# Right operands of a seven-product feed-forward made in four steps, memory's second product moved into the layer, down products over three banks

## The chip, the cores and the metric

The program runs on one core of one Trainium2 chip. The metric is the device time of one execution in microseconds (us); the figure for a kernel is the median of its runs. A core has five engines that work at the same time, each through its own list of instructions in the list's order: TensorE (PE in the profile; matrix products into PSUM banks), VectorE (DVE), ScalarE (ACT), GpSimd (POOL) and SyncE (SP, which issues DMA transfers here). An instruction starts when those before it on its engine have started and what it waits for is done, so one that waits holds up everything queued behind it.

## What is computed

A decoder of two layers over 512 tokens of width 1024, then a second block with sparse attention and retention, all in fp32. What the change touches is the feed-forward at the end of each of the two layers and the second of two small products on a "memory" of 256 rows:

```python
for i in range(DEPTH):                      # DEPTH = 2
    mem_kv = mem_n @ w_mem_kv[i]            # memory's product, 256 x 1024 by 1024 x 512
    ...                                     # layer 0: gated convolution, layer 1: banded attention
    x = x + jnp.concatenate([y_tok, y_mem], axis=-1) @ w_out
    h = rmsnorm(x, norm_ffn[i])
    x = x + (jax.nn.silu(h @ w_gate[i]) * (h @ w_up[i])) @ w_down[i]    # D_FF = 2816
return rmsnorm(x, final_norm)               # then second_block(...)
```

## The kernel before

**Precision.** Every fp32 operand is split in two: a rounded high part (`copy` on ACT, L70) and the difference (`lo_of` on DVE, L80). A product is three matmuls: high by high, low by high, high by low (`mm3`, L120 to L122). A weight tile arrives by DMA as raw fp32 (`wr`, 2 buffers), and becomes `wh` on ACT and `wl` on DVE (3 buffers each; `weights`, L103). A third matmul of a product waits for `wl`.

**Layout.** x stands as eight chunks of 128 features by 512 tokens. A block f of the feed-forward is 128 of the 2816 inner features: 22 blocks in groups of 4, 4, 4, 4, 3, 3 (`FFG`, L25).

**Plain blocks** (f = 0 to 4, `plain_gate_up`, L604): gate and up are two products of 24 matmuls by 512 columns each, into a `pp` and an `lg` bank. Behind them `z` (gate times the norm row R, DVE L73), silu on ACT, `u` (up times -R, DVE L76), `u*z` on POOL (L73), and the split into `acth`, `actl`. Block 0 also makes R from the sums of squares of x.

**Seven-product blocks** (f = 5 to 21, `gate_up`, L566): gate and up of a block and both halves of the tokens are taken as one 2 by 2 product, made with seven products of half the size (84 matmuls by 256 columns) instead of eight. It needs two sets of sums. The right operands, sums of the gained and normed x, are made once per layer (`halves`, L494): for each of four pairs of chunks two scaled chunks (`b`, DVE L76), four sums of 256 columns, one split of 256 and three of 512 columns (`B`, `Bh` on ACT; `Bl` and the like on DVE). The left operands are sums of the weights, made per block (`pair_weights`, L535: `a`, `s`). The seven products share three banks: U (`pp`, read in between by copies on ACT: `g`, `g`, `u`), Y and Z (`lg`).

**Down products.** The products with w_down of group g are spread over the blocks of group g+1, eight of them (four weight loads `i` by two output chunks `c`), called by `between` inside a block; those of the last group follow the loop. Each goes into a bank of the tag `tp` (2 banks) or `po` (1 bank) and is subtracted from x (DVE L638). Which block gets how many was `share` (L646): none before f = 4, then two each, and 3, 3, 2 in the groups of three blocks.

**Around it.** `run` (L1156) calls the feed-forward of layer 0, then the loads for a bias table, `mem_kv(1)` (memory's product for layer 1, L372) and the bias table, which ends in a broadcast of 2,304 KB through DRAM on POOL's queue (`band<-band`, L340). Then `layer_b` begins with two splits of each chunk of x (`gh`, `gl` and `g`), a sum of squares on POOL, and products with w_kv. After layer 1 `second` begins in a like way. The order of each engine's list is fixed at build time by a scheduler, which may put instructions of later code ahead.

Of the kernel before, what the change touches and what calls it, by code (L numbers as in the profile page):

```python
# [25 lines left out]
PLAIN = 5  # L26


class Build:
# [464 lines left out]
    def halves(self, x, R, gain):  # L494

        nc = self.nc
        tags = iter(["pa"] * 6 + ["pb"] * 10 + ["q"] * 4 + ["v"] * 8)
        spare = []  # L500

        def slot(name):
            tag = next(tags)
            if tag != "v":
                return self.slot(tag, F32R, name=name)
            if not spare:
                t = self.slot("v", F32R, (128, KWORDS), name)
                spare.extend([t[:, :512], t[:, 512:1024]])
            return spare.pop(0)

        sub = lambda out, a, b: nc.vector.tensor_tensor(out, a, b, op=ALU.subtract)
        sets = []
        for j in range(len(x) // 2):
            a, b, m, t = self.slot("t", name="b1"), self.slot("t", name="b2"), self.slot("s", name="m12"), self.slot("s", name="t34")
            for c, o in ((2 * j, a), (2 * j + 1, b)):
                self.stt(o, x[c], gain[:, c:c + 1], R, ALU.mult, ALU.mult)
            b11, b12, b21, b22, m1, m2, t3, m4 = (o[:, u:u + 256] for o in (a, b, m, t) for u in (0, 256))
            one = slot("B11")
            self.copy(one[:, :256], b11)
            self.lo_of(one[:, 256:], b11, one[:, :256])  # L520
            sub(m1, b11, b12)
            self.stt(m2, b22, -1.0, m1, ALU.mult, ALU.subtract)
            sub(t3, b22, b12)
            self.stt(m4, m2, -1.0, b21, ALU.mult, ALU.subtract)
            parts = []
            for o in (b, m, t):
                h, l = slot("Bh"), slot("Bl")
                self.copy(h, o)
                self.lo_of(l, o, h)
                parts.append(((h[:, :256], l[:, :256]), (h[:, 256:], l[:, 256:])))  # L530
            (p21, p22), (p1, p2), (p3, p4) = parts
            sets.append([(one[:, :256], one[:, 256:]), p21, p1, p2, p3, p22, p4])
        return [[s[i] for s in sets] for i in range(7)]

    def pair_weights(self, src):  # L535

# [28 lines left out]

    def gate_up(self, src, B, between):  # L566

        nc, w = self.nc, self.pair_weights(src)
        mm = nc.tensor.matmul
        b11, b21, m1, m2, t3, b22, m4 = B  # L570

        def product(ps, a, b, start):
            for j in range(4):
                (ah, al), (bh, bl) = (a[0][:, j], a[1][:, j]), b[j]
                mm(ps, ah, bh, start=start and j == 0, stop=False, skip_group_check=not start)  # L575
                mm(ps, ah, bl, start=False, stop=False, skip_group_check=not start)  # L576
                mm(ps, al, bh, start=False, stop=j == 3, skip_group_check=not start)  # L577

        U, Y, Z = (self.psum(t)[:, :256] for t in ("pp", "lg", "lg"))
        g, u = self.slot("t", name="g"), self.slot("t", name="u")[:, :256]  # L580
        g1, g2 = g[:, :256], g[:, 256:]
        add = lambda out, a, b: nc.vector.tensor_tensor(out, a, b, op=ALU.add)  # L582
        product(U, w["a11"], b11, True)
        self.copy(g1, U)
        product(Y, w["a12"], b21, True)
        add(g1, Y, g1)
        product(U, w["s2"], m2, False)
        self.copy(g2, U)
        product(Z, w["s1"], m1, True)
        product(U, w["s3"], t3, False)  # L590
        self.copy(u, U)
        add(u, Z, u)
        between(0)
        product(Z, w["s4"], b22, False)
        add(g2, Z, g2)
        nc.scalar.activation(g, g, AF.Silu)  # L596
        product(U, w["a22"], m4, False)
        between(1)
        act = self.slot("t", name="act")
        self.mul(act[:, :256], U, g1)  # L600
        self.mul(act[:, 256:], u, g2)
        return self.split(act, "b", name="act")
# [14 lines left out]
        self.mul(u, u, z, self.nc.gpsimd)  # L617
        return self.split(u, "b", name="act"), R

    def ffn(self, layer):  # L620
        nc, T = self.nc, self.T
        gain = self.gain(2 + layer)
        h = self.gained(self.x, gain)
        R = B = act = None

        def down(i, act, g):

            f0, f1 = FFG[g]
            n = f1 - f0
            w = []  # L630

            def one(c):
                if not w:
                    w.extend(self.weights(T["w_down"][layer, i][:, f0 * 256:f1 * 256], 2 * n, 128))
                ps = self.psum("po" if i % 2 else "tp")
                self.proj(ps, None, act, [t[:, c * n:c * n + n] for t in w])
                x = self.x[2 * i + c]
                nc.vector.tensor_tensor(x, x, ps, op=ALU.subtract)  # L638

            return [lambda: one(0), lambda: one(1)]  # L640

        for g, (f0, f1) in enumerate(FFG):
            last = act
            todo = [] if last is None else [p for i in range(4) for p in down(i, last, g - 1)]
            act = []
            share = -(-len(todo) // (f1 - max(f0, PLAIN - 1))) if todo else 0  # L646
            for f in range(f0, f1):
                mine = []
                if f >= PLAIN - 1:
                    mine, todo = todo[:share], todo[share:]  # L650

                def between(i):
                    for p in mine[i * (len(mine) // 2):] if i else mine[:len(mine) // 2]:
                        p()

                if f < PLAIN:
                    a, R = self.plain_gate_up(layer, f, h, R)
                    between(0)
                    between(1)
                    if f == 0:  # L660
                        B = self.halves(self.x, R, gain)
                else:
                    a = self.gate_up(T["w_gu"][layer, f - PLAIN], B, between)
                act.append(a)
        for i in range(4):
            for p in down(i, act, len(FFG) - 1):
                p()
# [488 lines left out]
    def run(self):  # L1156
        self.load_consts()
        self.mrs = None
        self.layer_a()
        self.ffn(0)  # L1160
        loaded = self.bias_loads()
        self.mem1 = self.mem_kv(1)
        self.bias_tables(loaded)
        self.layer_b()
        self.ffn(1)
        self.second()
# [123 lines left out]
```

## Time and profile before

| | |
|---|---|
| median of 3 runs | 1707.94 us (1705.91 to 1709.22) |
| the profiled execution, its own time | 1709.18 us |
| its span, first to last instruction | 1707.3 us |
| mean granted TensorE clock | 0.979 of full speed |
| PE busy | 1629.6 us, 95% of the span |
| DVE busy | 1253.8 us, 73% |
| ACT busy | 757.4 us, 44% |
| POOL busy | 193.7 us, 11% |

The profiled execution is one execution. Its own time is 1.9 us more than its span; the 1.9 us lie before the first and after the last instruction. A row of the timeline gives the start in us from the span's start, the duration, engine, line, operation and tiles, and in brackets how long the engine stood idle before it and what ended that. Matmuls overlap in the pipeline, so what one costs is the step from its start to the next start, not its duration; DVE's and ACT's overlap by some hundredths in the same way. Clock is the share of full speed that TensorE was granted.

### The profile page before, as it was taken

To read this page: it belongs to the slowest core of one execution; us is meant where nothing else is said; L and a number is where in the kernel's file an instruction comes from. 1 tells how busy PE (TensorE), PEld (TensorE's weight loads), DVE (VectorE), ACT (ScalarE), POOL (GpSimd) and SP (SyncE) were. 2 spreads that over 40 slices of the span, in tenths; PEclk is the share of its full clock that TensorE was granted. 3 is DMA by queue.
4 is the path that set the end of the run, shared out by engine and by line. 5 is a ranking of instruction groups with operands and counts; after the bars stand their busy time and mean duration, and the time that the engine had idled before them with its cause. 6 is when DMAs were issued, how large, how long until landed. Compare 5 with 4: busy or idle time off the path is not lost.

```text
span 1707.3 us, 24407 instructions
## 1 busy us (share of the span) xinstructions
PE 1629.6 (95%) x9408; PEld 1423.0 (83%) x9408; DVE 1253.8 (73%) x2330; ACT 757.4 (44%) x1404; POOL 193.7 (11%) x186
## 2 busy tenths in 40 slices
PE   8999979999999899997999999989899999999997
PEld 6888868999998678886899999967787888888887
DVE  7866776777777969977677777689878977764444
ACT  6532344444444557734344444434555633333333
POOL 1112310000000600050100000051001001010010
PEclk9999989999999899998999999999999999999999
DMA  5222222332324441221323322332512022243352
GB/s 196 87 86 96 90 69 92 104 107 92 114 85 120 131 164 64 81 86 61 105 95 101 110 99 93 97 122 87 162 56 67 17 91 82 84 138 123 113 165 87
DMA packets 51572, 171.60 MB, mean 101 GB/s; under 512 B 6680, under 2 KB 6880, under 8 KB 51328
## 3 DMA queue, kind: packets, MB, share of 16 engines
q1 hardware_dynamic: 45504, 151.11, 27.2%
q0 software_dynamic: 5376, 18.82, 3.2%
q8 instruction: 74, 1.21, 0.3%
q14 instruction: 42, 0.34, 0.1%
q10 hardware_dynamic: 576, 0.11, 0.0%
HBM read 160.56 MB, written 11.81 MB: 101 GB/s over the span
## 4 chain that ended last, share of the span: by engine, by line
PE 72%; DVE 15%; DMA 5%; issue 3%; ACT 3%; POOL 1%; DVEq 0%; SPq 0%; ACTq 0%; POOLq 0%
PE pp L122 7%; PE pp L121 7%; PE pp L120 6%; PE lg L120 4%; DVE wl L80 4%; PE lg L122 4%; PE lg L121 4%; PE po L120 3%; PE pp L575 3%; PE pp L577 3%; PE pp L576 3%; PE po L121 3%; PE po L122 3%; DMA wr<-in_w_gu_dram 3%; PE tp L262 2%
## 5 line engine op out<-in xcount | busy, mean ns | idle before, releaser
L70 ACT ACTIVATE wh<-wr 128x1024 fp32r<-128x1024 f32 (+3 forms) x246 | 251.9, 1024 | 376.6 <-PE pp L121 150.5
L80 DVE TENSOR_TENSOR wl<-wr,wh 128x1024 fp32r<-128x1024 f32 (+3 forms) x246 | 315.9, 1285 | 63.3 <-ACT wh L70 62.6
L120 PE MATMUL pp<-g,wh 128*128 128x512 f32 x592 | 235.8, 399 | 21.9 <-DVE z L73 14.0
L122 PE MATMUL pp<-g,wl 128*128 128x512 f32 x592 | 235.0, 397 | 7.9 <-DVE wl L80 7.8
L121 PE MATMUL pp<-g,wh 128*128 128x512 f32 x592 | 234.4, 396 | 0.3 <-DVE g L76 0.3
L120 PEld LDWEIGHTS pp<-g,wh 128*128 128x128 f32 x592 | 112.5, 190 | 44.4 <-ACT Bh L70 14.7
L122 PEld LDWEIGHTS pp<-g,wl 128*128 128x128 f32 x592 | 112.1, 189 | 31.0 <-DVE wl L80 10.3
L121 PEld LDWEIGHTS pp<-g,wh 128*128 128x128 f32 x592 | 112.5, 190 | 21.4 <-DVE g L76 1.0
L70 ACT ACTIVATE s<-s 128x512 fp32r<-128x512 f32 x136 | 85.0, 632 | 49.2 <-DVE s L555 46.4
L80 DVE TENSOR_TENSOR s<-s,s 128x512 fp32r<-128x512 f32 x136 | 90.1, 682 | 1.0 <-ACT s L70 0.8
L575 PE MATMUL pp<-Bh,s 128*128 128x256 f32 x272 | 78.8, 290 | 7.3 <-ACT g L70 7.0
L555 DVE TENSOR_TENSOR s<-wr,wr 128x512 f32<-128x512 f32 x68 | 46.8, 688 | 51.9 <-DMA wr<-in_w_gu_dram 51.9
L577 PE MATMUL pp<-Bh,s 128*128 128x256 f32 x272 | 78.0, 287 | 0.0
L577 PE MATMUL lg<-Bh,s 128*128 128x256 f32 x272 | 77.0, 283 | 0.0
L575 PE MATMUL lg<-Bh,s 128*128 128x256 f32 x272 | 76.9, 283 | 0.0
L120 PE MATMUL po<-acth,wh 128*128 128x512 f32 x176 | 70.7, 401 | 5.8 <-DVE x L638 5.8
L121 PE MATMUL po<-actl,wh 128*128 128x512 f32 x176 | 70.1, 398 | 0.0
L122 PE MATMUL po<-acth,wl 128*128 128x512 f32 x176 | 69.3, 394 | 0.0
L120 PE MATMUL tp<-acth,wh 128*128 128x512 f32 x176 | 68.9, 391 | 0.0
L121 PE MATMUL tp<-actl,wh 128*128 128x512 f32 x176 | 68.9, 391 | 0.0
L122 PE MATMUL tp<-acth,wl 128*128 128x512 f32 x176 | 68.5, 389 | 0.0
L596 ACT ACTIVATE g<-g 128x512 f32<-128x512 f32 x34 | 21.4, 631 | 100.9 <-DVE g L582 100.9
(503 smaller groups left out, 4650.9 us busy)
## 6 DMA issues: line engine op xcount, KB each, us to landing
wr<-in_w_gu_dram SPq DMA_DIRECT2D x68, 512.0 KB, 3.8
wr<-in_w_in_dram SPq DMA_DIRECT2D x44, 512.0 KB, 3.5
wr<-in_w_down_dram SPq DMA_DIRECT2D x32, 512.0 KB, 3.7
wr<-in_a_w_in_dram SPq DMA_DIRECT2D x18, 512.0 KB, 3.6
wr<-in_w_down_dram SPq DMA_DIRECT2D x16, 384.0 KB, 3.2
wr<-in_w_gate_dram SPq DMA_DIRECT2D x10, 512.0 KB, 3.4
wr<-in_w_up_dram SPq DMA_DIRECT2D x10, 512.0 KB, 3.4
wr<-in_a_w_out_dram SPq DMA_DIRECT2D x8, 512.0 KB, 3.5
```

Source lines behind the costliest of these rows:

```text
L70: self.nc.scalar.activation(out, in_, AF.Copy, scale=scale)
L80: self.nc.vector.tensor_tensor(out, x, hi.bitcast(F32), op=ALU.subtract)
L120: mm(ps, ah, bh, start=start, stop=False)
L121: mm(ps, ah, bl, start=False, stop=False)
L122: mm(ps, al, bh, start=False, stop=stop)
L262: self.nc.tensor.transpose(ps[:, c:c + 128], src, self.ident)
L555: nc.vector.tensor_tensor(t, a, b, op=ALU.add)
L575: mm(ps, ah, bh, start=start and j == 0, stop=False, skip_group_check=not start)
L576: mm(ps, ah, bl, start=False, stop=False, skip_group_check=not start)
L577: mm(ps, al, bh, start=False, stop=j == 3, skip_group_check=not start)
L596: nc.scalar.activation(g, g, AF.Silu)
```

## The change

Four edits, all in the feed-forward and in `run`. (1) `halves` becomes a generator: one pair of chunks per step, one step behind each of the plain blocks 1 to 4, instead of all four behind block 0. (2) The down products of the first group are spread 4, 2, 1, 1 over blocks 4 to 7 instead of 2, 2, 2, 2; in the groups of three blocks 2, 3, 3 instead of 3, 3, 2. (3) Their banks go `tp`, `tp`, `po` in turn instead of `tp`, `tp`, `po`, `po`. (4) `mem_kv(1)` with the bias table moves from behind the feed-forward of layer 0 to a place ahead of its last eight down products.

```diff
@@ halves
             sets.append([(one[:, :256], one[:, 256:]), p21, p1, p2, p3, p22, p4])
-        return [[s[i] for s in sets] for i in range(7)]
+            yield sets
@@ ffn
-    def ffn(self, layer):
+    def ffn(self, layer, between_last=None):
...
-                ps = self.psum("po" if i % 2 else "tp")
+                ps = self.psum("po" if (2 * i + c) % 3 == 2 else "tp")
...
-            share = -(-len(todo) // (f1 - max(f0, PLAIN - 1))) if todo else 0
-            for f in range(f0, f1):
-                mine = []
-                if f >= PLAIN - 1:
-                    mine, todo = todo[:share], todo[share:]
+            n = f1 - f0
+            shares = [0] * n if last is None else [4, 2, 1, 1] if f0 < PLAIN else [8 * (i + 1) // n - 8 * i // n for i in range(n)]
+            for f, share in zip(range(f0, f1), shares):
+                mine, todo = todo[:share], todo[share:]
...
                 if f < PLAIN:
                     a, R = self.plain_gate_up(layer, f, h, R)
+                    if f == 0:
+                        steps = self.halves(self.x, R, gain)
+                    else:
+                        sets = next(steps)
                     between(0)
                     between(1)
-                    if f == 0:
-                        B = self.halves(self.x, R, gain)
                 else:
+                    if f == PLAIN:
+                        B = [[s[i] for s in sets] for i in range(7)]
                     a = self.gate_up(T["w_gu"][layer, f - PLAIN], B, between)
                 act.append(a)
+        if between_last:
+            between_last()
         for i in range(4):
@@ run
         self.layer_a()
-        self.ffn(0)
-        loaded = self.bias_loads()
-        self.mem1 = self.mem_kv(1)
-        self.bias_tables(loaded)
+        def between():
+            loaded = self.bias_loads()
+            self.mem1 = self.mem_kv(1)
+            self.bias_tables(loaded)
+
+        self.ffn(0, between)
```

What this does to the lists of the engines, at three places. First DVE's list in the plain blocks of layer 0, before: behind `u` of block 0 (here `u_1805`) all of `halves` follows, of which these are the first rows; `wl` is the difference of a weight tile, `actl` that of the block's result.

```order
L76 SCALAR_TENSOR_TENSOR u_1805<-lg_1774,Rf_345_1769 128x512
L76 SCALAR_TENSOR_TENSOR b_354_1812<-x_81,gains,Rf_345_1769 128x512
L76 SCALAR_TENSOR_TENSOR b_355_1813<-x_82,gains,Rf_345_1769 128x512
L511 TENSOR_TENSOR m_356_1814<-b_354_1812 128x256
L511 TENSOR_TENSOR t_357_1815<-b_355_1813,b_354_1812 128x256
L76 SCALAR_TENSOR_TENSOR m_356_1814<-b_355_1813,m_356_1814 128x256
L80 TENSOR_TENSOR wl_1983<-wr_1981,wh_1982 128x1024
L80 TENSOR_TENSOR actl_1809<-u_1805,acth_1808 128x512
```

Of the 41 rows between that `u` and `z` of block 1, 39 are of `halves`. The same list with the change, behind block 1's gate:

```order
L73 TENSOR_TENSOR z_1843<-pp_1812,Rf_345_1769 128x512
L80 TENSOR_TENSOR wl_1946<-wr_1944,wh_1945 128x1024
L76 SCALAR_TENSOR_TENSOR u_1877<-lg_1846,Rf_345_1769 128x512
L76 SCALAR_TENSOR_TENSOR b_366_1884<-x_81,gains,Rf_345_1769 128x512
L76 SCALAR_TENSOR_TENSOR b_367_1885<-x_82,gains,Rf_345_1769 128x512
L80 TENSOR_TENSOR actl_1881<-u_1877,acth_1880 128x512
L80 TENSOR_TENSOR B_370_1890<-b_366_1884,B_370_1890 128x256
```

Between `u` of a block and `z` of the next there stand now ten rows of one step, the block's `actl` and one `wl`, and a second `wl` behind that `z`. POOL's list has one instruction in each of these blocks, `u*z`.

Second, ACT's list around the first seven-product block of layer 0 (f = 5). Before, `g_2264` twice and `u_2265` are the copies out of bank U, and `wh_2402`, `a_477`, `s_479` and so on the left operands of block 6:

```order
L70 ACTIVATE wh_2332<-wr_2331 128x1024
L70 ACTIVATE wh_2402<-wr_2398 128x1024
L70 ACTIVATE g_2264<-pp_2261 128x256
L70 ACTIVATE a_477_2406<-wr_2399 128x512
L70 ACTIVATE s_479_2411<-s_478_2409 128x512
L70 ACTIVATE g_2264<-pp_2261 128x256
L70 ACTIVATE s_481_2416<-s_480_2414 128x512
```

With the change the left operands that stand around the copies are those of block 5 itself:

```order
L70 ACTIVATE s_458_2277<-s_457_2275 128x512
L70 ACTIVATE s_460_2282<-s_459_2280 128x512
L70 ACTIVATE g_2298<-pp_2295 128x256
L70 ACTIVATE s_462_2287<-s_461_2285 128x512
L70 ACTIVATE s_464_2292<-s_463_2290 128x512
L70 ACTIVATE g_2298<-pp_2295 128x256
L70 ACTIVATE wh_2366<-wr_2365 128x1024
L70 ACTIVATE u_2299<-pp_2295 128x256
L70 ACTIVATE wh_2436<-wr_2432 128x1024
L70 ACTIVATE a_482_2440<-wr_2433 128x512
```

`a_482`, the first that needs block 6's second raw tile, has moved behind all three copies.

Third, SP's list at the end of layer 0's feed-forward; before, the four loads of the last down products stand ahead of memory's weights (the last of the four is the second row):

```order
L355 DMA mem_5252<-in_mem_dram 128x512
L111 DMA wr_5214<-in_w_down_dram 128x768
L111 DMA wr_5275<-in_w_mem_k_dram 128x1024
L111 DMA wr_5318<-in_w_mem_k_dram 128x1024
L111 DMA wr_5360<-in_w_mem_v_dram 128x1024
L111 DMA wr_5366<-in_w_mem_v_dram 128x1024
```

With the change the four stand behind them, and the loads of w_kv still last:

```order
L111 DMA wr_5254<-in_w_mem_v_dram 128x1024
L111 DMA wr_5344<-in_w_down_dram 128x768
L111 DMA wr_5372<-in_w_down_dram 128x768
L111 DMA wr_5400<-in_w_down_dram 128x768
L111 DMA wr_5428<-in_w_down_dram 128x768
L111 DMA wr_5581<-in_w_kv_k_dram 128x1024
```

The last rows of memory's product on PE now stand ahead of the last eight down products, and the broadcast of the bias table ahead of the copies of x on POOL.

## Rows read from the trace of the kernel before

**Rows 1.** The page, part 1: busy us, share of the span, instructions of each engine.

```profile
PE 1629.6 (95%) x9408; PEld 1423.0 (83%) x9408; DVE 1253.8 (73%) x2330; ACT 757.4 (44%) x1404; POOL 193.7 (11%) x186
```

**Rows 2.** Timeline of PE, layer 0, plain blocks 1 to 4.

```profile
227.64 0.39 PE L121 MATMUL lg<-g,wh 128*128 128x512 f32 x1
235.00 0.77 PE L120 MATMUL pp<-g,wh 128*128 128x512 f32 x1 [6.97 <-DVE z L73]
...
238.59 0.79 PE L122 MATMUL lg<-g,wl 128*128 128x512 f32 x1 [2.40 <-DVE wl L80]
...
244.31 0.50 PE L120 MATMUL lg<-g,wh 128*128 128x512 f32 x1
...
251.49 0.39 PE L120 MATMUL lg<-g,wh 128*128 128x512 f32 x1
...
262.37 0.39 PE L120 MATMUL lg<-g,wh 128*128 128x512 f32 x1
```

**Rows 3.** Windows: length, busy PE, PEld, DVE, ACT, POOL; clock, DMA share, GB/s.

```profile
235.00:245.00 10.00, 7.60 (x18) 5.52 (x19) 6.50 (x7) 2.78 (x4) 1.26 (x1) 0.52 0.34 105
```

**Rows 4.** Timeline of PE, layer 1, the same place as rows 2.

```profile
802.13 0.76 PE L120 MATMUL pp<-g,wh 128*128 128x512 f32 x1 [6.98 <-DVE z L73]
```

**Rows 5.** Timeline of PE, first seven-product block, layer 0; last row layer 1.

```profile
278.75 0.28 PE L576 MATMUL lg<-Bh,s 128*128 128x256 f32 x1
278.88 0.28 PE L577 MATMUL lg<-Bh,s 128*128 128x256 f32 x1
281.84 0.41 PE L575 MATMUL pp<-Bh,s 128*128 128x256 f32 x1 [2.69 <-ACT g L70]
...
287.68 0.28 PE L575 MATMUL lg<-Bh,s 128*128 128x256 f32 x1
...
848.60 0.54 PE L575 MATMUL pp<-Bh,s 128*128 128x256 f32 x1 [2.37 <-ACT g L70]
```

**Rows 6.** Timeline of DVE inside `halves`, layer 0: steps from start to start.

```profile
228.43 0.41 DVE L76 SCALAR_TENSOR_TENSOR t<-m,b 128x256 f32<-128x256 f32 x1
228.76 0.68 DVE L80 TENSOR_TENSOR Bl<-m,Bh 128x512 fp32r<-128x512 f32 x1
229.37 0.74 DVE L76 SCALAR_TENSOR_TENSOR b<-x,gains,Rf 128x512 f32<-128x512 f32 x1
230.03 0.68 DVE L80 TENSOR_TENSOR Bl<-t,Bh 128x512 fp32r<-128x512 f32 x1
```

**Rows 7.** Timeline of POOL and of DVE, a plain block's `u*z` and the `wl` beside it.

```profile
236.20 1.26 POOL L73 TENSOR_TENSOR u<-u,z 128x512 f32<-128x512 f32 x1 [19.63 <-DVE u L76]
...
236.57 1.97 DVE L80 TENSOR_TENSOR wl<-wr,wh 128x1024 fp32r<-128x1024 f32 x1
```

**Rows 8.** The page, part 6: DMA issues, KB each, median us from issue to landing.

```profile
wr<-in_w_gu_dram SPq DMA_DIRECT2D x68, 512.0 KB, 3.8
```

**Rows 9.** Waits of PE, 500 to 612 us: us in total, times, longest.

```profile
PE po L120 <- DVE x L638: 4.2, 3, 1.7
...
PE pp L142 <- ACT wh L70: 2.8, 1, 2.8
PE pp L575 <- ACT g L70: 0.9, 1, 0.9
```

**Rows 10.** Windows as rows 3: the ends of the feed-forwards of layers 0 and 1.

```profile
547.30:592.20 44.90, 36.96 (x185) 31.09 (x184) 43.73 (x59) 26.76 (x46) 27.47 (x31) 0.89 0.42 136
...
1114.00:1150.90 36.90, 28.38 (x117) 22.47 (x116) 34.38 (x35) 12.34 (x16) 24.04 (x25) 0.91 0.39 139
```

**Rows 11.** Groups by line, 547 to 612 us: count, busy us, mean ns, idle before.

```profile
L76 DVE SCALAR_TENSOR_TENSOR g<-x,gains,g 128x512 fp32r<-128x512 f32 x8 | 11.9, 1505 | 0.0
```

**Rows 12.** Waits of PE, 1080 to 1165 us, as rows 9.

```profile
PE pp L122 <- DVE wl L80: 7.0, 1, 7.0
```

**Rows 13.** Timeline of ACT, the copy of w_kv's second tile; DMA issues, 590 to 612 us.

```profile
607.81 1.06 ACT L70 ACTIVATE wh<-wr 128x1024 fp32r<-128x1024 f32 x1 [7.99 <-DMA wr<-in_w_kv_v_dram]
...
band<-band POOLq DMA_DIRECT2D x1, 2304.0 KB, 13.3
```

## The prediction

> **What bounds the kernel now.** I began with the page's first part, the busy time of each engine: PE is busy 1629.6 of 1707.3 us [rows 1], with 9408 matmuls. The change leaves out no matmul and adds none, so it can only act on what PE loses: waits, and slow matmuls after a wait. So I went through PE's timeline for steps longer than usual, and then for each to the engine that ended the wait. Full speed is a matmul of 512 columns every 0.227 us: a plain block, 48 of them, takes 262.37 − 251.49 = 10.88 us [rows 2]. One of 256 columns takes 278.88 − 278.75 = 0.13 us, some 0.12 where many follow each other [rows 5]. Four places that the change touches stand out: the plain blocks, the first seven-product block, and the ends of the two feed-forwards.
>
> **The plain blocks.** In layer 0 PE waits 6.97 us for `z` and then 2.40 us for `wl` [rows 2]. `z` is one short operation; it is late because DVE's list has all of `halves` ahead of it. After the wait the granted clock is 0.52 over 10 us, the lower of the two levels (1.2 of 2.4 GHz) [rows 3]. From 227.64 to 244.31 there are 16 matmuls in 16.67 us; at full speed they take 16 × 0.227 = 3.6. Lost: 13.0 us, of it 9.4 waits and some 3.6 slow matmuls. Layer 1 has the same wait, 6.98 us [rows 4], and I take the same loss: 26.0 in all.
>
> Is that covered when the steps are spread? DVE's work between two plain blocks is then one step: 2 `b` at 0.66, 5 operations of 256 columns at 0.33, 3 of 512 at 0.61 [rows 6], together 1.3 + 1.7 + 1.8 = 4.8 us. The block's own are `z`, `u`, `actl` at 0.61 and two `wl` of double that size, 2 × 1.22: 4.3 us. The sum of 9.1 is less than PE's 10.88. One `wl` beside POOL's `u*z` takes 1.97 instead of 1.22 [rows 7], 0.75 more, so 9.8; if DVE also stands still for all of an `u*z`, 1.26 [rows 7], 10.4 without the longer `wl`. It still fits, if narrowly. The fourth step lies beside four down products. Term: **−26.0**, with bounds −26 and, if two more operations are held by 0.75 in each block (11.9 against 10.9), −18 (the first rival). I take the full term, since POOL has a single instruction in a plain block.
>
> **The first seven-product block.** From 278.88 to 287.68 there are 8.80 us [rows 5] for 13 steps of 0.12 and 12 of 0.227, 4.3 us: lost 4.5. The wait in it, 2.69, is for a copy `g` of bank U on ACT, which stood behind left operands of the next block that had to be loaded first. Layer 1 has 2.37 there [rows 5]; I take 4.5 again. With the change those operands stand behind the three copies. Something else is late instead. Four down products now lie ahead of the block, and the fourth subtraction from x stands in DVE's list ahead of the sum `s_461`, which must be done before a raw buffer is free for the next w_down tile. That is five operations from the block's start, 5 × 0.61 = 3.0 us; the load takes 3.8 like its neighbours [rows 8], the copy `wh` 1.06 [rows 13]: 7.9 us. PE comes to that down product after five products, 5 × 12 × 0.12 = 7.2. Wait: 0.7. The next blocks have one down product ahead instead of two, 12 × 0.227 = 2.7 us less cover for the same chain; how late they get is between 0 and 2.7, and I take the middle, 1.4. Left 2.1 of 4.5, so −2.4 per layer, **−4.7** for both (bounds 0 and −9).
>
> **Later groups.** In the first block of a group of three PE waits 0.9 us for `g` [rows 9], once in each layer. Shares 2, 3, 3 take one down product out of that block, and the copies come earlier in ACT's list: **−1.8** (bounds 0 and −1.8).
>
> **The end of layer 0.** Here PE waits in many small places, 4.2 us for x in the bank `po` [rows 9] among them, and three banks in turn look like the cure. But from the last seven-product block to the start of `layer_b` DVE is busy 43.73 of 44.90 us, PE 36.96 [rows 10]. DVE sets the end there. The change takes none of its operations away, so waits for `po` come back as others: nothing for the banks. I count four smaller things. Memory's loads, four w_mem tiles and the memory itself, pass the last four w_down loads in SP's list; each issue waits for a raw buffer, so this costs only if the broadcast stands in between, which is the second rival. One more down product, 9 × 0.227 = 2.0, lies ahead of the last group, less the 0.6 of its subtraction: −1.4. The second tile of w_kv no longer lands behind the 13.3 us broadcast [rows 13], where PE waited 2.8 [rows 9]: −2.8. Against that PE gets a longer idle stretch ahead of the last downs, and its clock may fall: the nearest row cost 3.6 [rows 3]; here the wait is shorter, so +2.0. DVE's operations on memory's tiles wait for DMA, which it now does ahead of its busiest stretch: +1.2. Sum **−1.0** (bounds −5 and +4).
>
> **The end of layer 1.** DVE is busy 34.38 of 36.90 us [rows 10] and PE waits 7.0 for a `wl` [rows 12] behind it. No work leaves DVE: **0** (bounds ±3).
>
> **Sum.** −26.0 − 4.7 − 1.8 − 1.0 = −33.5 against the profiled 1709.2, which is 1.2 above the median of the runs: 1674.5 against that median, rounded to **1675**. The forecast's own range is 1669 to 1682, mostly from the two seven-product terms and the end of layer 0.
>
> **Rivals.**
>
> *The delay moves to the next blocks.* If operations of a step are held as that `wl` was [rows 7], two more in each block, DVE needs 11.9 us for a block that PE does in 10.9: 1.0 late, over four steps in two layers 8 us. Time 1683. For it: DVE has only 0.5 to 1.8 us of slack. Against: one POOL instruction per block. Chance 0.14.
>
> *The last w_down tile lands behind the broadcast.* The broadcast is issued as soon as memory's product is done, and w_down's last loads are now issued about then. Before, ACT's copy of w_kv's second tile came after an idle time of 7.99 us that its DMA ended, beside a broadcast of 13.3 [rows 13]. A w_down tile that has to wait like that comes 13.3 − 3.8 = 9.5 late, and with PE's other products used up most of it is paid: 1684 to 1685. Chance 0.11. The Trainium skill, "DMA: Bandwidth & Descriptors", section "Queues, rings and completion order", says that a DMA engine takes turns between the queues that have work, packet by packet; by that a tile beside the broadcast would take about twice its 3.8 us [rows 8], not the whole broadcast, an estimate by which this rival's time would be 1679. The idle time of 7.99 [rows 13] speaks against so mild a price here.
>
> *The ends do pay.* DVE's eight `g` at the start of `layer_b` take 1505 ns each [rows 11] while POOL is busy with squares (27.47 us in that stretch [rows 10]); the like with one output takes 0.74 [rows 6]. POOL's squares and the DMA issues stand in another order with the change. If DVE escapes them, 8 × 0.77 = 6.1 us come free there, and half of that at the other end, where POOL is busy 24.04 [rows 10]: 1666. Chance 0.12.
>
> *The plain blocks get slower (the other side).* As `u*z` stretched a `wl` by 0.75 [rows 7], POOL or ACT's traffic could hold every operation of a step, 13 in a block with the block's own: 9.8 + 9.1 = 18.9 us a block, 8 more than PE's 10.9, in three blocks of each layer 48 us: 1675 + 48 = 1723, slower than before. It decides from 33 / 6 = 5.6 us late per block, a DVE cycle of 16.5. Against: POOL works 1.26 us per plain block [rows 7], and it cannot hold DVE for longer than that. The Trainium skill, "SBUF — State Buffer", section "Who interferes with whom", says that a DVE operation with two inputs from SBUF and a GpSimd operation that reads SBUF exclude each other, the one issued first keeping the other out for its whole length; by that rule the price is at most one `u*z` per block, and the 0.75 above [rows 7] agrees. Chance 0.03.
>
> *The change doesn't do what it says.* The scheduler could have drawn the four steps together again; then nothing of the 26 is won, and the rest lies within 1700 to 1708. The lists show the steps apart. Chance 0.02.
>
> **How the numbers follow.** Forecast 0.56, the rivals 0.14, 0.11, 0.12, 0.03 and 0.02; 0.02 for what I don't see. The range 1664 to 1689 takes in the forecast's own range, the rival below it and the two above it with some room each. A difference of 0.2%, 3.4 us, is about what a measurement of this kernel can tell from none. Faster by more: 0.94; within it 0.03; slower 0.03.
>
> **What would show it.** Right: no wait of several us for `z` in blocks 1 to 4 of either layer, with the clock near full; waits of about 1 us for w_down's `wh` in the first seven-product block in place of 2.7 for `g`; the waits for `po` gone at layer 0's end, yet DVE's busy time there much the same; the 7.0 us wait at the end of layer 1 back at nearly its size. Wrong: `z` or `wl` late by 1 us or more in every plain block (first rival), a w_down tile that lands with the end of the broadcast (second), `g` at much under 1.5 us (third). If the plain blocks gain less than 20 us, the central step is wrong.

## The result and the profile after

The changed kernel takes 1685.5 us (median of 4 runs, 1682.5 to 1686.7) beside 1706.9 us for the one before on the same chip: ratio 0.987, 95% interval 0.985 to 0.989. That is faster by 21.5 us, where the forecast's centre was 33. It lies inside the stated range, 1664 to 1689, but outside the forecast's own, 1669 to 1682.

The page of the changed kernel, part 1, for comparison with [rows 1]: PE has 10 us less busy time with the same 9408 matmuls; the mean granted clock is 0.987 instead of 0.979.

```profile
PE 1619.6 (96%) x9408; PEld 1415.5 (84%) x9408; DVE 1248.2 (74%) x2330; ACT 756.6 (45%) x1404; POOL 196.4 (12%) x186
```

Windows of the changed kernel over the plain blocks 0 to 4 of layer 0; columns as in [rows 3]:

```profile
211.00:222.00 11.00, 11.00 (x50) 9.10 (x49) 4.94 (x6) 5.20 (x6) 1.29 (x1) 1.00 0.28 94
222.00:233.00 11.00, 11.00 (x50) 9.11 (x49) 10.10 (x15) 5.38 (x8) 1.67 (x1) 1.00 0.14 43
233.00:244.00 11.00, 11.00 (x50) 9.10 (x49) 10.10 (x15) 5.38 (x8) 1.65 (x1) 1.00 0.30 97
244.00:255.00 11.00, 11.00 (x50) 9.12 (x49) 10.10 (x15) 5.38 (x8) 1.65 (x1) 1.00 0.30 98
```

PE is busy for all of every window at full clock, where before it stood for 7 us and then ran at 0.52 [rows 2, 3]. DVE is busy 10.1 of 11.0 us in each block that carries a step.

The waits of PE of the changed kernel, layer 0 from 205 to 540 us and layer 1 from 760 to 1088 us, plain and seven-product blocks together:

```profile
PE pp L575 <- ACT g L70: 1.5, 2, 1.0
PE tp L120 <- ACT wh L70: 1.0, 1, 1.0
...
PE pp L575 <- ACT g L70: 1.9, 2, 1.7
PE tp L120 <- ACT wh L70: 1.3, 1, 1.3
PE pp L575 <- ACT u L70: 1.2, 2, 0.7
```

No wait for `z` is left, and the 2.7 for `g` in the first seven-product block [rows 5] has gone. Smaller waits stand in its place, in several blocks.

The ends of the two feed-forwards: PE's waits from 531 to 600 us and from 1088 to 1140 us, and windows, for comparison with [rows 9, 10, 12].

```profile
PE tp L174 <- DVE acc L166: 10.9, 1, 10.9
PE pp L122 <- DVE wl L80: 1.4, 1, 1.4
...
PE pp L122 <- DVE wl L80: 8.2, 1, 8.2
PE tp L120 <- DVE x L638: 3.3, 2, 2.2
...
531.40:588.90 57.50, 43.42 (x220) 36.03 (x219) 49.68 (x83) 28.68 (x49) 31.23 (x34) 0.85 0.54 177
...
567.90:579.20 11.30, 0.36 (x3) 0.01 (x1) 11.30 (x12) 3.97 (x7) 11.27 (x14) 0.64 0.34 136
579.20:588.90 9.70, 8.32 (x25) 6.90 (x26) 6.83 (x21) 1.06 (x1) 0.78 (x2) 0.54 0.66 220
1087.90:1134.40 46.50, 34.94 (x146) 28.01 (x145) 36.52 (x63) 13.42 (x18) 24.71 (x25) 0.85 0.37 127
```

At the end of layer 0 the many small waits have given way to one of 10.9 us, for the sum of squares (`acc`) behind the last subtraction from x. In its window DVE is busy 11.30 of 11.30 us and POOL 11.27; DVE's busy time holds stretches in which POOL keeps it waiting (f2_add_dve below). After it PE runs at a clock of 0.54. At the end of layer 1 the wait for `wl` is 8.2 instead of 7.0.

**Where the time went, by stage.** To compare kernels whose lists differ, I took from each profile the length of a stage and subtracted its matmuls at full speed: those of 512 columns at 0.2267 us, of 256 at 0.1178, the others nearly in proportion. For instance, from the matmul that spreads the norm row (209.05 us) to the first of the seven products (265.76) the changed kernel has 247 matmuls of 512 columns, 56.0 us; the stage takes 56.7, so PE lost 0.7. Before, 223 of them (50.6 us) took 64.5: lost 13.9. "Plain" is that stage in both layers; "seven" runs on to the last matmul of the seven products, both layers; "end 0" from there to the norm row of layer 1's feed-forward, so with `layer_b`; "end 1" from layer 1's last seven-product matmul to the last matmul of the program. The absolute sizes of the last three have little meaning, and much of "end 1" is code that no kernel here changes, except as noted; differences under 2 us in the two ends are not read. One profile each: that of e3_shares is of the slowest of six executions, 5.4 us above their median, and those of g2_sums, g3_f1sums and h4_both lie 3 above theirs. Medians and ratios are from all executions. A ratio is to the kernel before as it ran beside that kernel; its median was 1706.9 us beside the change and 1708.5 to 1708.8 beside the experiments, so where a few us matter the ratios are to be compared.

| kernel | median us | ratio to before, 95% interval | plain | seven | end 0 | end 1 |
|---|---|---|---|---|---|---|
| before | 1706.9 | | 27.7 | 19.8 | 36.1 | 60.5 |
| the change | 1685.5 | 0.987, 0.985 to 0.989 | 1.5 | 21.7 | 36.0 | 62.0 |
| e1_steps | 1692.0 | 0.990, 0.989 to 0.992 | 1.5 | 29.5 | 36.9 | 59.8 |
| e2_nosteps | 1708.4 | 1.000, 0.999 to 1.001 | 26.0 | 19.7 | 34.9 | 61.6 |
| e3_shares | 1695.4 | 0.993, 0.991 to 0.995 | 1.5 | 28.9 | 39.9 | 63.7 |
| e4_mem | 1683.4 | 0.986, 0.983 to 0.988 | 1.5 | 22.8 | 33.7 | 61.6 |
| e5_banks | 1681.0 | 0.984, 0.983 to 0.986 | 1.5 | 19.9 | 32.7 | 63.4 |
| g2_sums | 1680.0 | 0.983, 0.982 to 0.985 | 1.5 | 15.5 | 35.6 | 64.3 |
| f1_sq_act | 1675.3 | 0.981, 0.980 to 0.983 | 1.5 | 21.0 | 29.4 | 56.7 |
| f2_add_dve | 1675.5 | 0.981, 0.979 to 0.982 | 1.5 | 21.5 | 31.8 | 55.1 |
| g3_f1sums | 1671.0 | 0.978, 0.977 to 0.979 | 1.5 | 17.2 | 31.4 | 56.9 |
| h2_banks | 1670.7 | 0.978, 0.976 to 0.979 | 1.5 | 16.9 | 29.7 | 58.2 |
| h3_mem | 1667.5 | 0.976, 0.975 to 0.977 | 1.5 | 16.6 | 27.1 | 57.8 |
| h4_both | 1672.4 | 0.979, 0.978 to 0.980 | 1.4 | 17.5 | 32.5 | 57.6 |

Against before the change won 26.2 in "plain", lost 2.0 in "seven", won 0.1 in "end 0" and lost 1.5 in "end 1": 22.8 together, beside 22.4 between the two spans. So the forecast's largest term came out, and the 6.5 that it gave to the seven-product blocks did not. The question is why.

Inside "seven", the length of a block is the time from its first matmul into U to that of the next block, on PE's timeline. Undisturbed, a block with two down products takes 15.6 us, one with a single down product 2.7 less, 12.8. The blocks 5 to 10, in layer 0 and in layer 1:

| kernel | 5 | 6 | 7 | 8 | 9 | 10 |
|---|---|---|---|---|---|---|
| before | 20.1, 19.9 | 15.6, 15.6 | 15.6, 15.6 | 15.6, 15.6 | 15.6, 15.6 | 15.6, 15.6 |
| the change | 17.2, 17.5 | 13.5, 13.7 | 13.3, 13.8 | 15.6, 15.6 | 16.8, 19.0 | 16.3, 15.6 |
| e1_steps | 22.8, 23.2 | 15.8, 15.8 | 15.6, 15.6 | 15.8, 16.1 | 16.9, 16.8 | 15.6, 15.6 |
| e2_nosteps | 19.2, 19.4 | 13.5, 13.8 | 13.0, 13.0 | 15.6, 15.6 | 15.6, 15.6 | 15.6, 15.6 |
| g2_sums | 17.2, 17.1 | 13.2, 13.4 | 13.7, 13.2 | 15.6, 15.6 | 15.6, 15.6 | 15.6, 15.6 |

For the 19.0, for instance, these two rows of the changed kernel:

```profile
879.36 0.28 PE L575 MATMUL pp<-B,wh 128*128 128x256 f32 x1
...
898.40 0.28 PE L575 MATMUL pp<-B,wh 128*128 128x256 f32 x1
```

### The profile page after: what moved, and what is told of

It reads as the page before. It is cut to its first block, busy times and chain, and to the rows that moved or that the text cites. A ratio compares the mean times of both kernels' runs of the same rounds, so it can differ in the third digit from the quotient of the medians.

```text
span 1684.9 us, 24388 instructions
## 1 busy us (share of the span) xinstructions
PE 1619.6 (96%) x9408; PEld 1415.5 (84%) x9408; DVE 1248.2 (74%) x2330; ACT 756.6 (45%) x1404; POOL 196.4 (12%) x186
## 3 DMA queue, kind: packets, MB, share of 16 engines
q1 hardware_dynamic: 45504, 151.11, 27.1%
## 4 chain that ended last, share of the span: by engine, by line
PE 71%; DVE 15%; DMA 7%; ACT 3%; issue 3%; POOL 1%; SPq 0%; DVEq 0%; ACTq 0%; POOLq 0%
PE pp L122 8%; PE pp L121 8%; PE pp L120 8%; PE lg L120 4%; PE lg L121 4%; PE lg L122 4%; DMA wr<-in_w_gu_dram 3%; DVE wl L80 3%; PE pp L575 3%; PE pp L576 2%; PE pp L577 2%; PE tp L262 2%; PE tp L120 2%; PE tp L121 2%; PE tp L122 2%
## 5 line engine op out<-in xcount | busy, mean ns | idle before, releaser
L80 DVE TENSOR_TENSOR wl<-wr,wh 128x1024 fp32r<-128x1024 f32 (+3 forms) x246 | 305.6, 1243 | 70.1 <-ACT wh L70 68.8
L122 PEld LDWEIGHTS pp<-g,wl 128*128 128x128 f32 x592 | 112.2, 189 | 33.7 <-DVE wl L80 13.0
L120 PE MATMUL tp<-acth,wh 128*128 128x512 f32 x264 | 104.4, 396 | 5.7 <-DVE x L638 3.3
L121 PE MATMUL tp<-actl,wh 128*128 128x512 f32 x264 | 104.0, 394 | 0.0
L122 PE MATMUL tp<-acth,wl 128*128 128x512 f32 x264 | 103.4, 392 | 0.0
L120 PEld LDWEIGHTS tp<-acth,wh 128*128 128x128 f32 x264 | 50.0, 190 | 16.4 <-ACT wh L70 2.6
L122 PEld LDWEIGHTS tp<-acth,wl 128*128 128x128 f32 x264 | 50.0, 190 | 10.6
L638 DVE TENSOR_TENSOR x<-x,tp 128x512 f32<-128x512 f32 x72 | 49.2, 683 | 12.6 <-PE tp L122 12.6
L576 PE MATMUL lg<-Bl,s 128*128 128x256 f32 x204 | 58.1, 285 | 0.0
```

The source lines that it names most:

```text
L80: self.nc.vector.tensor_tensor(out, x, hi.bitcast(F32), op=ALU.subtract)
L120: mm(ps, ah, bh, start=start, stop=False)
L121: mm(ps, ah, bl, start=False, stop=False)
L122: mm(ps, al, bh, start=False, stop=stop)
```

## The experiments

**e1_steps: edit 1 alone.** The change with edits 2 to 4 undone.

```diff
-                ps = self.psum("po" if (2 * i + c) % 3 == 2 else "tp")
+                ps = self.psum("po" if i % 2 else "tp")
...
-            shares = [0] * n if last is None else [4, 2, 1, 1] if f0 < PLAIN else [8 * (i + 1) // n - 8 * i // n for i in range(n)]
+            shares = [0] * n if last is None else [2, 2, 2, 2] if n == 4 else [3, 3, 2]
...
-        self.ffn(0, between)
+        self.ffn(0)
+        loaded = self.bias_loads()
+        self.mem1 = self.mem_kv(1)
+        self.bias_tables(loaded)
```

> Edit 1 alone: halves in four steps, all else as before. If the steps bring what the forecast gave them (26) and need nothing of the other edits: 1681. If the fourth step and the sums of the first seven-product block need four down products as cover and get two (5.4 us instead of 10.9), PE waits there some 2 to 3 us per layer: 1684 to 1687, the plain blocks 1 to 4 still without a wait of several us.

Measured: 1692.0. The plain blocks win the same 26.2 as in the change, but the seven-product blocks lose 9.7 more than before. The waits of PE in layer 0 and the place of the largest, in this kernel:

```profile
PE lg L575 <- ACT s L70: 3.5, 1, 3.5
PE pp L575 <- ACT g L70: 1.8, 3, 0.9
...
266.69 0.58 PE L575 MATMUL lg<-Bh,s 128*128 128x256 f32 x1 [3.50 <-ACT s L70]
```

The first seven-product block waits 3.5 us for its own left operand `s`: on DVE the fourth step and the sums of that block lie between the last plain block and the third product that PE comes to, and two down products are 5.4 us of cover for them. Block 5 takes 23 us, 3 more than before. The mechanism is the second case of the expectation; its size was set too low, since 3.5 us and further waits for `g` come together, the clock behind the long wait is 0.72 over 9.3 us (from 266.7), and blocks 8 and 9 are late too.

**e2_nosteps: edits 2 to 4 alone.**

```diff
-                    if f == 0:
-                        steps = self.halves(self.x, R, gain)
-                    else:
-                        sets = next(steps)
                     between(0)
                     between(1)
+                    if f == 0:
+                        sets = list(self.halves(self.x, R, gain))[-1]
```

> Edits 2 to 4 alone: halves in one piece behind block 0. By the forecast's sum the other edits bring 7.5: 1699. By the two traces, stage by stage, they bring nothing or cost 1 to 4: 1707 to 1711. A wait of 7 us for z in block 1 of either layer as before.

Measured: 1708.4, ratio 1.000. Without the steps the other three edits do nothing that can be told from zero; "seven" is 19.7 as before. In layer 0 the wait for `z` is back, and the one for `g` in the first seven-product block is 1.9:

```profile
PE pp L120 <- DVE z L73: 7.0, 1, 7.0
PE lg L122 <- DVE wl L80: 2.4, 1, 2.4
PE pp L575 <- ACT g L70: 1.9, 1, 1.9
```

**e3_shares: the change with the old shares.** The shares of e1_steps, nothing else.

> The change with the old shares 2, 2, 2, 2 and 3, 3, 2. By the forecast the new shares bring 6.5: 1692. By the traces the seven-product stages of the two layers lost 2.0 with the change: if that is the shares' own loss, 1683 to 1685; if the new shares repair what the steps cost in the first seven-product block, 1688 to 1692, with waits of 2 to 3 us there.

Measured: 1695.4. "Seven" loses 28.9, 7.2 more than with the new shares, and the wait of e1_steps is there again:

```profile
268.35 0.38 PE L575 MATMUL lg<-Bh,s 128*128 128x256 f32 x1 [3.49 <-ACT s L70]
```

So the new shares repair what the steps break: "seven" gains nothing from them without the steps (e2_nosteps, where edits 3 and 4 are in as well) and 7 us with them. The two ends came out 5.6 worse than in the change as well, although nothing in them was edited but the group of three ahead of them. This profile is of an execution 5.4 us slower than the median, so how much of the 5.6 is the edit's, and why the median lies above the expected 1688 to 1692, stays open.

**g2_sums: the change, with a raw buffer freed earlier.** The same operations in another order of writing.

```diff
-        put("a12", a12)
-        s1 = put_sum("s1", a21, a22)
-        s2 = put_sum("s2", s1, a11)
-        put_sum("s3", a11, a21)
-        put_sum("s4", s2, a12)
+        s1 = plus("s1", a21, a22)
+        s2 = plus("s2", s1, a11)
+        s3 = plus("s3", a11, a21)
+        put("a12", a12)
+        put("s1", s1)
+        put("s2", s2)
+        put("s3", s3)
+        put("s4", plus("s4", s2, a12))
```

(`plus` is the addition into a slot `s` that `put_sum` began with.) The chain in question, in the changed kernel around block 9 of layer 0 (from 325.25 us), from DVE's, SP's, ACT's and PE's timelines:

```profile
323.39 0.69 DVE L555 TENSOR_TENSOR s<-wr,wr 128x512 f32<-128x512 f32 x1
...
324.14 0.33 SPq L111 DMA_DIRECT2D wr<-in_w_down_dram  x1
...
327.93 1.06 ACT L70 ACTIVATE wh<-wr 128x1024 fp32r<-128x1024 f32 x1 [1.86 <-DMA wr<-in_w_down_dram]
328.89 0.36 ACT L70 ACTIVATE g<-pp 128x256 f32<-128x256 f32 x1
...
329.31 0.38 PE L575 MATMUL pp<-Bh,s 128*128 128x256 f32 x1 [1.03 <-ACT g L70]
```

The third sum ends, the load of the w_down tile is issued, lands 3.8 us later, its copy `wh` runs on ACT, and only then the copy `g` that stands behind it there, for which PE waits 1.0.

> The change with the sums s1, s2, s3 of pair_weights written ahead of the splits, so that the raw buffer a w_down tile waits for comes free some 1.5 us earlier; same operations. If the waits for g (3.4 us) and wh in the seven-product blocks come from the chain sum, raw buffer, load of w_down, wh, g: they shrink and the time falls by 2 to 5 us, 1680 to 1683. If ACT's list or the clock makes them: no change, 1685.

Measured: 1680.0. "Seven" falls from 21.7 to 15.5, below what it was before the change, and the blocks 9 and 10 are undisturbed in both layers. In this kernel the same load is issued 7.1 us ahead of block 9 (which starts at 326.06) instead of 1.1, and `g` waits for nothing but PE:

```profile
318.96 0.33 SPq L111 DMA_DIRECT2D wr<-in_w_down_dram  x1
...
327.75 0.39 ACT L70 ACTIVATE g<-pp 128x256 f32<-128x256 f32 x1 [0.53 <-PE pp L579]
```

So the chain over two raw buffers makes the waits of blocks 9 and 10. It is late only in kernels that have the steps: in e2_nosteps, with the change's shares, the load is issued 8.4 us ahead of block 9 (330.90 and 339.26):

```profile
330.90 0.33 SPq L111 DMA_DIRECT2D wr<-in_w_down_dram  x1
```

Why the steps, all done by block 5, leave the chain late four blocks on was not taken apart.

**e4_mem: memory's product back behind the feed-forward.** The last hunk of e1_steps alone.

> The change with memory's second product and the bias table back behind the feed-forward of layer 0. By the forecast this edit was worth 1 us; by the traces the end of layer 0 with the stage behind it is 0.1 shorter with the change, all four edits together. DVE bounds that end either way: 1684 to 1688, with w_kv's second tile again behind the broadcast (PE waits near 2.8 for its wh) and less waiting for the norm's sum. If the 10.9 us wait for the sum is this edit's own cost, 1678 to 1682.

Measured: 1683.4, between the two cases expected; the interval overlaps the change's, so the move is not shown to be worth anything here. "End 0" is 2.3 shorter without it. PE's waits from 531 to 600 us:

```profile
PE tp L144 <- DVE wl L80: 2.8, 2, 1.7
PE pp L142 <- DVE k L73: 2.6, 1, 2.6
...
PE tp L174 <- DVE mv L76: 1.3, 1, 1.3
```

The 10.9 us wait for the sum (L174) is gone, though the three banks are still there. The loads came out as expected. DMA issues from 545 to 615 us, first in the changed kernel, then in this one:

```profile
band<-band POOLq DMA_DIRECT2D x1, 2304.0 KB, 12.5
...
wr<-in_w_kv_v_dram SPq DMA_DIRECT2D x2, 512.0 KB, 4.5
```

```profile
band<-band POOLq DMA_DIRECT2D x1, 2304.0 KB, 12.4
...
wr<-in_w_kv_v_dram SPq DMA_DIRECT2D x2, 512.0 KB, 12.0
...
579.15 1.73 SPq L111 DMA_DIRECT2D wr<-in_w_kv_v_dram  x2
...
578.72 0.56 POOL L340 DMA_DIRECT2D band<-band  x1 [1.50 <-DMA band<-s]
```

And PE waits for them, by way of ACT's list:

```profile
591.36 1.06 ACT L70 ACTIVATE wh<-wr 128x1024 fp32r<-128x1024 f32 x1 [13.39 <-DMA wr<-in_w_kv_v_dram]
592.33 0.58 ACT L70 ACTIVATE Rb<-tp 128x512 f32<-128x512 f32 x1
...
593.60 0.68 DVE L73 TENSOR_TENSOR k<-pp,Rb 128x512 f32<-128x512 f32 x1
...
594.34 0.39 PE L142 MATMUL pp<-wh,gh 128*128 128x256 f32 x1 [2.57 <-DVE k L73]
```

The norm row `Rb` stands in ACT's list behind the copy of the late tile, `k` needs `Rb`, and the product with w_kv waits for `k`: 2.57 us, close to the 2.8 before [rows 9].

Two tiles issued 0.4 us and more behind the broadcast take 12.0 us, as long as the broadcast itself, against 3.8 for such a tile by itself [rows 8]. The DMA queues from 581 to 589 us in this kernel, q0 with the broadcast and q1 with the tiles (packets, MB, share of the 16 engines):

```profile
q0 software_dynamic: 102, 1.88, 59.8%
q1 hardware_dynamic: 88, 0.36, 31.9%
```

The tiles move 88 packets beside 102 of the broadcast, but of 4.1 KB against 18.4 each, so they get a sixth of the bytes; the other 0.69 MB of their 1.05 follows from 589 to 592 us, when the broadcast is done. The Trainium skill, "DMA: Bandwidth & Descriptors", section "Queues, rings and completion order", has the engines take turns between queues packet by packet; the trace agrees. What failed is my estimate of twice 3.8 from it, which took the turns to be of equal size.

**e5_banks: the old banks.** The first hunk of e1_steps alone.

> The change with the old banks (tp, tp, po, po). If three banks in turn only move waits at DVE-bound ends: within 3 us of the change, 1683 to 1688. If they are what keeps the single downs of the later blocks from waiting: 1690 or more, with waits for po of 4 to 6 us as before.

Measured: 1681.0, ratio 0.984 (0.983 to 0.986) beside 0.987 (0.985 to 0.989): some 5 us faster than the change, with intervals that just meet. I had expected a difference of at most 3 us, or a loss. PE's waits from 525 to 600 us and one window over the end of layer 0:

```profile
PE po L120 <- DVE x L638: 4.0, 3, 2.2
PE pp L121 <- DVE gl L76: 3.0, 3, 2.1
...
531.00:590.00 59.00, 50.42 (x244) 40.82 (x244) 51.57 (x84) 29.17 (x51) 30.99 (x34) 0.91 0.56 182
```

The waits for `po` are back and there are three for `gl`, none over 2.2 us. The clock over this end is 0.91, in the change 0.85. DVE is busy nearly all the time in both (51.57 of 59.00 and 49.68 of 57.50).

So the 10.9 us wait needs edits 3 and 4 together. Where both are in, PE waits for the sum 10.9 us (the change), 9.8 (e2_nosteps), 11.3 (e3_shares) and 9.7 (g2_sums). With three banks but not the move (e4_mem) its longest wait in "end 0" is 2.6, with the move but not three banks (e5_banks) 2.2, with neither 2.8 (before) and 2.7 (e1_steps). Nor are the old waits only gathered into one: summed over "end 0" PE waits (idle stretches of more than 0.1 us on its timeline) 12.1 us before, 14.3 in the change, 10.8 in e4_mem and 9.0 in e5_banks, while what that stage loses beside its waits is 24.0, 21.7, 22.9 and 23.7. So against the kernels with one of the two edits the change's end loses by waiting longer, not by the clock behind the wait. Why the two edits do this together was not taken apart.

**f1_sq_act: the squares of the norms on ACT instead of POOL,** on the change.

```diff
-            if not first and c < last:
-                nc.gpsimd.tensor_tensor(sq, x, x, op=ALU.mult)
-            else:
-                nc.scalar.activation(sq, x, AF.Square)
+            nc.scalar.activation(sq, x, AF.Square)
```

> The change with the squares of the norms' sums on ACT instead of POOL (the sums stay on POOL). If DVE bounds the ends of the feed-forwards and is held there by POOL's work (g 1.5 us instead of 0.74), about half of the holds go: g falls to 0.8 to 1.1 us at layer 0's end, and the time to 1677 to 1682. If the chain of the sum of squares is not what PE waits for at 568 us, or ACT's list gets in its own way: 1685 to 1688.

Measured: 1675.3, ratio 0.981. That is below the 1677 to 1682 expected, and `g` (below) falls further than foreseen. "End 0" loses 6.6 less than in the change and "end 1" 5.3 less.

**f2_add_dve: the running sums on DVE as well.** On f1_sq_act:

```diff
-                (nc.vector if first or c == last else nc.gpsimd).tensor_tensor(acc, acc, sq, op=ALU.add)
+                nc.vector.tensor_tensor(acc, acc, sq, op=ALU.add)
```

> f1_sq_act with the norms' running sums on DVE too, so POOL has nothing left in the norms. If the remaining holds by POOL's additions cost more than 7 additions of 0.61 = 4.3 us per norm: g falls to about 0.75 us and the time to 1670 to 1675. If not: DVE, the bound of the ends, has 4.3 us more to do, 1676 to 1682.

Measured: 1675.5, no different from f1_sq_act. DVE's groups by line from 540 to 612 us, in the change, in f1_sq_act and in f2_add_dve (columns as in [rows 11]):

```profile
L76 DVE SCALAR_TENSOR_TENSOR g<-x,gains,g 128x512 fp32r<-128x512 f32 x8 | 10.4, 1305 | 0.0
L76 DVE SCALAR_TENSOR_TENSOR gl<-x,gains,gh 128x512 fp32r<-128x512 f32 x8 | 9.7, 1215 | 0.8 <-ACT gh L70 0.8
```

```profile
L76 DVE SCALAR_TENSOR_TENSOR gl<-x,gains,gh 128x512 fp32r<-128x512 f32 x8 | 9.4, 1178 | 0.8 <-ACT gh L70 0.8
L76 DVE SCALAR_TENSOR_TENSOR g<-x,gains,g 128x512 fp32r<-128x512 f32 x8 | 5.9, 741 | 0.0
```

```profile
L76 DVE SCALAR_TENSOR_TENSOR gl<-x,gains,gh 128x512 fp32r<-128x512 f32 x8 | 6.0, 748 | 0.8 <-ACT gh L70 0.8
L76 DVE SCALAR_TENSOR_TENSOR g<-x,gains,g 128x512 fp32r<-128x512 f32 x8 | 6.0, 747 | 0.0
```

With the squares off POOL `g` falls from 1305 to 741 ns, with the sums off it `gl` from 1178 to 748. The second step gives DVE back 8 × 0.43 = 3.4 us and costs it additions of about 0.6 us each, so it comes out even. The Trainium skill, "SBUF — State Buffer", section "Who interferes with whom", says that a DVE operation with two SBUF inputs and a GpSimd operation that reads SBUF exclude each other; these two runs agree: each group comes down to 741 to 748 ns once the POOL operation beside it is gone.

**The combinations.** g3_f1sums has the diffs of f1_sq_act and g2_sums; h2_banks, h3_mem and h4_both have in addition those of e5_banks, of e4_mem, and of both.

> Squares on ACT and the sums of pair_weights first, together, on the change. The two act in different stages, so the gains of 10 (ends, and the norms) and about 6 (seven-product blocks) against the change should add up to most of 16: 1669 to 1673. If an end that comes out of the scheduler otherwise takes some of it back: 1673 to 1677.

> As g3_f1sums, with the old banks tp, tp, po, po. If the old banks are better in themselves by the 5 us that e5_banks showed: 1664 to 1668. If that gain was the scheduler's other order at the ends, which the squares have emptied anyway: within 2 us of g3_f1sums.

> As g3_f1sums, with memory's second product behind the feed-forward again. If the move is worth its 2.8 us (w_kv's tile not behind the broadcast) once DVE is less full: 2 to 4 us slower than g3_f1sums. If it stays what e4_mem showed: the same or up to 3 us faster.

> As g3_f1sums, with memory's second product back and the old banks: edits 1 and 2 alone, with squares and sums. If edits 3 and 4 bring nothing: no slower than g3_f1sums, 1664 to 1672. If they carry 2 us or more together: 1673 or more.

Measured: g3_f1sums 1671.0, so of two gains from different stages, 10.2 and 5.5 against the change, 14.5 are left together. h2_banks 1670.7: once the squares have left POOL, the old banks win nothing more, as in its second case. h3_mem 1667.5, a ratio of 0.976 (0.975 to 0.977): with memory's product where it was before, the kernel is faster by 3.5 us (the intervals still overlap by a hair), and it is the fastest that was run, 41 us under the kernel before. h4_both 1672.4, between its two cases: had the two effects added, it would lie near 1667. Its "end 0" loses 5.4 more than that of h3_mem, of which up to 3 are this slower execution's. The same pattern stands in both series of "end 0": with neither of edits 3 and 4 it loses 36.9 (e1_steps) and 32.5 (h4_both), with the three banks alone 33.7 (e4_mem) and 27.1 (h3_mem), with the move alone 32.7 (e5_banks) and 29.7 (h2_banks), with both 36.0 (the change) and 31.4 (g3_f1sums). Each seems to help without the other and not beside it; one profile each, and why is not settled.

## Why the prediction was right where it was, and where it failed

- **The plain blocks: right in mechanism and size.** Forecast −26.0, measured −26.2, and DVE's 10.1 us per block (busy time, with the small overlap of neighbours) lie within the 9.1 to 10.4 that the sum gave against PE's 10.9. e1_steps shows that this gain is edit 1's alone. The first rival and the one of the other side are out: at full clock without a wait there is no lateness to pass on.
- **The seven-product blocks: the step that failed.** The forecast had −4.7 for the first such block and those behind it, and −1.8 for the later groups; measured was +2.0 for all of "seven". By the table of blocks, both layers together: block 5 won 2.9 + 2.4 = 5.3, where 4.5 less a wait of 0.7 in each had been 7.6; the wait for the tile's `wh` that was foreseen is there, 1.0 and 1.3, but others stand beside it. Blocks 6 and 7 lost 2.9, where 1.4 in each layer had been 2.8. The later groups won about 1. And blocks 9 and 10 lost 5.5, for which the forecast had nothing: it let the lateness end with the blocks that have little cover. g2_sums shows what it is, since the raw buffer freed earlier takes just these 5.5 away.
- **What edit 2 is for was seen only by half.** The forecast put the fourth step beside four down products and costed it at nothing; that held. But the four products were counted as a gain against before as well, and e1_steps, e3_shares and e2_nosteps show them to be a repair: with two in their place "seven" loses 7 to 8 us more, and without the steps they bring nothing.
- **The end of layer 0: right that it would bring nothing, but its terms did not come as summed, so the near zero is luck.** Forecast −1.0, measured −0.1. DVE sets the end, as said: f1_sq_act frees it of POOL's squares and wins 6.6 there, where undoing the move wins 2.3 and undoing the banks 3.3. f1_sq_act shortens POOL's part of the sum as well, but f2_add_dve, which takes POOL out of the sum wholly, wins nothing more; that speaks for DVE. The term of −2.8 for w_kv's tile is right as a wait: with the move undone 2.57 of it come back. But the forecast took the idle stretch that stands against it to be shorter than the 7 us in the plain blocks; it is 10.9, where the move and the three banks come together, and that was not foreseen. The term of +2.0 for the clock is not borne out: the ten us behind the long wait ran at 0.54, yet beside its waits this end loses 2.3 less than before. PE waits 2.2 more there, and the two cancel.
- **The end of layer 1:** forecast 0, measured +1.5, the 7.0 us wait being 8.2; within the stated 3.
- **The rivals.** "The ends do pay": `g` only fell from 1.5 to 1.3 us with the change, 1.6 us in all, and the end kept its length. Its mechanism was the right one, though: where an edit really takes POOL's squares away it is worth 10 us. "The last w_down tile behind the broadcast" did not happen, if only just: the last of them was issued at 549.14 us and landed 3.3 later, the broadcast was issued at 552.84. The time, 1685.5, is nearly what this rival had named, by another cause. That the change would do nothing was out with the first window.
- **The total:** the spans differ by 22.4 where the sum had 33.5: of the 11 that are missing, 8.5 lie in the seven-product blocks and 2.4 in the two ends. The time stayed inside the stated range by the room left in it for rivals whose mechanism did not come, and that is luck; the largest term, 26.0 of the 33.5, came as it was worked out. So did the signs named beforehand: no wait for `z`, 1.0 and 1.3 us for `wh` in place of the 2.7 for `g`, no wait for x in `po` at layer 0's end, 8.2 us at layer 1's. Two slips of rounding in the sum, 4.7 for twice 2.4 and 1674.5 for 1707.94 − 33.5, change nothing.

## What to carry to other kernels

When work is spread from one block over several, its last piece meets the block that follows: look there for the cover, and don't count as a gain what only repairs. Behind such a place, follow the loads through their buffers for some blocks more: a chain through two buffers can come up late well after the work that made it late. And where one engine is full to the end of a stage, edits that give the others more room can undo each other there: two that make no long wait alone made one together, so run each without the other. The larger gain came from easing what held the full engine up.

## What the runs showed that I had not expected

- Two edits made a wait together that neither makes alone: 10.9 us with three banks and the move, at most 2.6 in "end 0" with either of them.
- A tile of 512 KB issued 0.4 us behind a broadcast of 2304 KB on another queue took 12.0 us, the broadcast 12.4. It had its turns, 88 packets beside 102, but packets of 4.1 KB against 18.4.
- POOL held DVE's `g` and `gl` at 1.6 to 1.8 times their length, each by another of its operations: 1305 to 741 ns without the squares, 1178 to 748 without the sums.
